# Cached keys fetched page by page and scored with full-height products in a hybrid decoder step

## The chip, the cores and the metric

The kernel runs on one core of a Trainium2 chip. The time is device microseconds (us) from the start of the program to its end, for one execution, with one launch. The core has five engines that run side by side, each through its own instruction queue in order: PE (TensorE, matmuls; PEld is its weight load), DVE (VectorE), ACT (ScalarE), POOL (GpSimd) and SP (SyncE). SP, ACT and POOL also issue DMAs; a queue that issues is written SPq, ACTq or POOLq. An indirect DMA (a gather, one row of memory per partition by a list of indices) is issued by POOL in this kernel.

## The reference

One inference step of a one-layer decoder, with a prompt group (512 tokens) and a sample group (8 sequences of 4 new tokens with 2,048 cached positions each, in 16 pages of 128). The part that the change touches is the sparse attention of the sample group:

```python
ki_past = cki[page_table].reshape(DB, PAST_LEN, IDX_DIM)          # indexer keys, 16 pages a sequence
sc = index_scores(qi, wi, concat([ki_past, ki_new]))               # sum over 8 heads of relu(qi . ki) * wi
_, idx = lax.top_k(sc, 256)                                        # 256 positions of 2,052
k_sel, v_sel = gather(ck, cv by page_table and idx)                # cached keys and values, 2 heads of 64
o = softmax(q . k_sel / 8) @ v_sel                                 # 8 query heads, 4 for each key head
```

Around it stand a gated MLP, the same attention for the prompt, an attention over 256 memory rows, and an expert layer with 16,384 experts (the last two thirds of the time). Everything is in float32; the large projections are three products of halves in a rounded format (fp32r), which are written `mm3`.

## The kernel before, in words

**Phase A** (the first 400 us of the trace) makes the projections, the prompt's attention and the sample group's attention. The projections are the main line: 19 weight tiles of 512 KB (`wA`), each loaded by SP (L232), cut by ACT (L220) and DVE (L224) into a high and a low half, and multiplied on PE (L256 to L258). Two raw tiles and two pairs of halves are held. The other work of phase A runs as *sides*: generators that the main line steps by a declared time, which gives the order in which the program is written. The order on each queue is then drawn by a planner of the tile framework, which plays the program through on a timeline: at every moment a free engine takes the earliest-written instruction that is ready. A buffer of a ring is given out by the planner at the moment its first writer is placed. Once drawn, the order of each queue is fixed, and a queue waits in order.

**Index pages.** The indexer keys of a sequence are 16 pages. `index_rows` (L1317 to L1327) issues four pairs of pages behind each weight tile on SP: a register load (L1324) and a DMA of 32 KB (L1326) for each page, 128 of them in 16 weight tiles. The pages of sequences 4 and 5 and of 6 and 7 lie in two slots of the ring `kv` of three slots; the rest in another ring.

**Index scores.** `sample_scores` multiplies the pages (L1366), and after the sequences 5 and 7 it calls `fetch_kv`, which takes the slot that has come free. Behind that follow the scores of the new positions (L1374 to L1379) and two masks on POOL (L1381, L1382). `sample_select` (L1388) then finds the 256th largest score by 32 rounds of counting on DVE (L1419 to L1431, the count itself is L1420).

**Cached keys and values.** `fetch_kv` fills a slot of the ring `kv` (128 x 2,048, three slots) with the keys of one sequence (the first eight calls) or the values (the last eight), by four gathers of 128 rows of 2 KB (L1283). A row of `cK` is one (head, quarter of 16) of a page: four chunks `e` of the head dimension with 128 positions each. One gather brings four pages, 32 partitions each.

**Scores.** `sample_keys` (L1464 to L1510) runs over the eight sequences: DVE builds the queries spread over four chunks (L1495), PE makes sixteen products on 64 x 64 quarters of the array (L1502), with two PSUM banks, and ACT copies the two banks out (L1506). Behind each sequence stands the next `fetch_kv`. `sample_attend` (L1514) adds the mask of the selected positions (L1541 to L1543), takes the softmax, and multiplies with the values (L1559). Its end closes the memory of the sample group, in which the second half of the prompt's stream is then laid out; so it is a join.

Of the kernel before, what the change touches and what calls it, by code (L numbers as in the profile page):

```python
# [18 lines left out]
P = 128  # L19
NP = 512  # L20
NS = 32
# [30 lines left out]
class Kernel:  # L52
# [173 lines left out]
    def wtile(self, pool, src, kt=KT, n=P):  # L226

        more = pool is self.pw and self.gp is not None and self.RX
        if more:
            self.raws = (self.raws + 1) % (2 + self.RX)  # L230
        raw = self.t(self.gp, [P, kt, n], tag="wraw", bufs=self.RX) if more and self.raws > 1 else self.t(pool, [P, kt, n], tag="wraw", bufs=2)
        load = self.nc.sync.dma_start(raw, src)  # L232
        self.loads += 1
        if self.todo and self.loads > 2:
            self.index_rows(load)
        hi = self.t(pool, [P, kt, n], F32R, tag="whi", bufs=2)
        lo = self.t(pool, [P, kt, n], F32R, tag="wlo", bufs=2)
        self.split(hi, lo, raw)
        return hi, lo


# [1026 lines left out]
    def fetch_kv(self, s2):  # L1268
        n = len(self.kv)
        if n < 16:  # L1270
            kv = self.t(s2, [P, 2048], tag="kv", bufs=self.RING)
            kv = kv.rearrange("p (m x) -> p m x", m=4)
            for m in range(4):
                self.gather(kv[:, m, :], self.I["cV" if n >= 8 else "cK"], self.s_ix[:, n * 4 + m : n * 4 + m + 1])
            self.kv.append(kv)

    RING = 3
# [8 lines left out]
    def pages(self, s1, s2):  # L1286
        nc, I = self.nc, self.I

        pid = self.t(s1, [P, 1])
        for r in range(0, P, 32):  # L1290
            nc.gpsimd.iota(pid[r : r + 32], [[0, 1]], base=0, channel_multiplier=1, allow_small_or_imprecise_dtypes=True)
        pt_i = self.t(s1, [P, P], I32)
        nc.gpsimd.dma_start(pt_i, I["page_table"].rearrange("b n -> (b n)").partition_broadcast(P))
        pf = self.t(s1, [P, P])
        nc.vector.tensor_copy(pf, pt_i)
        self.s_ix = self.t(s1, [P, 64], I32)
        tmp = self.t(s1, [P, 64])
        for u in range(4):
            r = slice(u * 32, u * 32 + 32)

            nc.vector.tensor_scalar(tmp[r, :32].rearrange("p (b c f) -> p b c f", c=2, f=2),
                                    pf[r].rearrange("p (b c v r f) -> p v r b c f", c=2, v=2, r=2, f=2)[:, u % 2, u // 2],
                                    32.0, pid[r], ALU.mult, ALU.add)
            nc.vector.tensor_scalar(tmp[r, 32:], pf[r].rearrange("p (n u) -> p u n", u=4)[:, u], 32.0, pid[r], ALU.mult, ALU.add)
# [12 lines left out]
    def index_rows(self, behind):  # L1317
        nc = self.nc
        src = self.I["cI"].rearrange("(n d) x -> n d x", d=64)
        with self.tc.issue_after(getattr(behind, "ins", behind)):  # L1320
            for pt_i, b, m in self.todo[: self.PAGES]:
                for c in range(2):
                    n = b * 16 + 2 * m + c
                    page = nc.values_load(pt_i[:1, n : n + 1], engines=[mybir.EngineType.SP], min_val=0, max_val=src.shape[0] - 1,  # L1324
                                          skip_runtime_bounds_check_because="a page table holds pages of the pool")
                    nc.sync.dma_start(self.rows[b][c * 64 : c * 64 + 64, m, :], src[bass.ds(page, 1)].rearrange("n d x -> (n d) x"))  # L1326
        self.todo = self.todo[self.PAGES :]  # L1327

    PAGES = 4


    def sample_scores(self, s1, s2):
# [131 lines left out]
    def sample_keys(self, s1, s2):  # L1464
        nc = self.nc

        qb = self.s_qb = self.t(s2, [P, 8, 2, 4, 4])
        nc.vector.memset(qb, 0.0)
        for g in range(2):
            r = slice(g * 64, g * 64 + 64)  # L1470
            for q in range(4):
                nc.vector.tensor_scalar(qb[r, :, g, q], self.s_q[r, q].rearrange("p (b t) -> p b t", t=4), 0.125, None, ALU.mult)

        qs = self.t(s2, [P, 4, 8, 16])
        self.s_room = Room(qs.rearrange("p e b q -> p (e b q)"))
        ps = self.pst("pb")
        for e in range(4):
            perm = self.t(s1, [P, P], tag="qst", bufs=2)
            nc.vector.tensor_copy(perm.rearrange("p (u g d) -> p u g d", u=4, g=2),
                                  self.ident.rearrange("p (g e d) -> p e g d", g=2, e=4)[:, e].unsqueeze(1).to_broadcast([P, 4, 2, 16]))  # L1480
            nc.tensor.matmul(ps[:, e * P : e * P + P], perm, self.s_q.rearrange("p r t -> p (r t)"), start=True, stop=True)
        for e in range(4):
            nc.scalar.activation(qs[:, e].rearrange("p b (r t) -> p r b t", r=4), ps[:, e * P : e * P + P].rearrange("p (r b t) -> p r b t", r=4, b=8),
                                 AF.Copy, scale=0.125)

        own = self.t(s2, [P, 4])
        nc.vector.tensor_reduce(own, self.ident.rearrange("p (r c d) -> p c r d", r=2, d=16), AX.XY, ALU.add)
        yield 1.0
        while not self.indexed:
            yield 1.0  # L1490
        S = [self.t(s1, [P, 4, 512], tag="S8", bufs=2) for _ in range(2)]
        self.s_S = [S[b // 4][:, b % 4, :] for b in range(8)]
        for b in range(8):
            q4 = self.t(s2, [P, 4, 64], tag="q4", bufs=2)
            nc.vector.tensor_tensor(q4.rearrange("p e (c q) -> p e c q", c=4), qs[:, :, b].unsqueeze(2).to_broadcast([P, 4, 4, 16]),  # L1495
                                    own.unsqueeze(1).unsqueeze(3).to_broadcast([P, 4, 4, 16]), ALU.mult)

            pair = [self.pst("pb") for _ in range(2)]
            for e in range(4):
                for o, ps in zip((0, 64), pair):  # L1500
                    for c in range(2):
                        nc.tensor.matmul(ps[c * 64 : c * 64 + 64, : 2 * P].rearrange("p (f x) -> p f x", f=2), q4[o : o + 64, e],  # L1502
                                         self.kv[b][o : o + 64, 2 * c : 2 * c + 2, e * P : e * P + P], start=e == 0, stop=e == 3,
                                         skip_group_check=True, tile_position=(o, c * 64))
            for r, ps in enumerate(pair):
                nc.scalar.copy(self.s_S[b].rearrange("p (m r f x) -> p r f m x", m=4, r=2, f=2)[:, r],  # L1506
                               ps[:, : 2 * P].rearrange("p (f m x) -> p f m x", f=2, m=4))
            self.fetch_kv(s2)
            yield 4.0 * self.SK
        self.keyed = True  # L1510
# [3 lines left out]
    def sample_attend(self, s2, s1):  # L1514
        nc, I = self.nc, self.I
        sel, qb = self.s_sel, self.s_qb
# [38 lines left out]
        def values(b, A):  # L1555
            po = self.pst("pb")
            for m in range(4):
                for c in range(4):
                    nc.tensor.matmul(po[c * NS : c * NS + NS, :P], A[:, m, c, :], self.kv[8 + b][:, c, m * P : m * P + P],  # L1559
                                     start=m == 0, stop=m == 3)  # L1560
# [16 lines left out]
        ps = self.pst("pb")  # L1577
# [4 lines left out]
        A = turn(nxt)  # L1582
        partn = self.t(s1, [P, 2, P], tag="qst", bufs=2)
        for b in range(8):
# [4 lines left out]
            if b == 0:  # L1589
                ps = self.pst("pb")  # L1590
# [3 lines left out]
            if b < 7:  # L1594
                A = turn(nxt)
# [281 lines left out]
```

## Time and profile before

| | |
|---|---|
| median of 3 runs | 1784.9 us (1784.82 to 1789.05) |
| the profiled execution: its own time | 1789.2 us |
| its span in the trace | 1787.5 us |
| mean granted clock of TensorE | 0.959 |
| PE busy | 1661.1 us, 93% |
| DVE busy | 1481.7 us, 83% |
| ACT busy | 864.8 us, 48% |
| POOL busy | 490.4 us, 27% |
| DMA | 460.33 MB, mean 258 GB/s |

The profile is of one execution. Busy time of an engine leaves out the instructions that issue DMAs from SP and ACT, register loads and waits. Matmuls overlap, so a busy PE isn't a PE at its peak. The granted clock is the share of 2.4 GHz that the chip gave PE: 1.0 is 2.4 GHz and 0.5 is 1.2 GHz. A bracket such as `[13.80 <-PE t L1502]` in a timeline says how long the engine had been idle before the instruction and what ended the idle time.

### The profile page before, as it was taken

The numbers are of one execution on the slowest core, as the hardware profiler recorded it, in microseconds if no ns is written. First come the engines' busy times: TensorE is split into PE (matmuls) and PEld (weight loads), VectorE is DVE, ScalarE is ACT, GpSimd is POOL, SyncE is SP. The second block draws the span as 40 slices with busy tenths as digits, with TensorE's granted clock in tenths as the row PEclk, the third lists the DMA queues.
The fourth block names the chain that finished last, engine by engine and source line by source line (L and its number), as shares of the span: only waits on it lengthen the run. The fifth ranks groups of instructions, "written<-read, shape, count | busy, mean of one in ns | idle before, by whom it ended". The sixth has DMA issues, their size and how long they took to land.

```text
span 1787.5 us, 29611 instructions
## 1 busy us (share of the span) xinstructions
PE 1661.1 (93%) x10238; PEld 1465.2 (82%) x10238; DVE 1481.7 (83%) x3654; ACT 864.8 (48%) x1585; POOL 490.4 (27%) x437
## 2 busy tenths in 40 slices
PE   6999989889997998899899998999999999999995
PEld 5879757679886997789889988788788888888884
DVE  4486889755759999999999885799898988878887
ACT  4345776655553335664775674333343333333333
POOL 2100133130000053323223222244333534335343
PEclk8999779889998999899999999999999999999998
DMA  5423436346854597989689789799998999999986
GB/s 178 133 64 111 127 97 200 108 149 212 254 178 122 158 340 267 344 313 344 231 285 312 250 298 299 258 358 331 362 353 302 373 357 325 355 330 323 362 301 234
DMA packets 195205, 460.33 MB, mean 258 GB/s; under 512 B 17976, under 2 KB 98616, under 8 KB 193648
## 3 DMA queue, kind: packets, MB, share of 16 engines
q1 hardware_dynamic: 132928, 241.63, 40.5%
q0 software_dynamic: 53072, 207.71, 32.8%
q10 hardware_dynamic: 9056, 9.11, 1.6%
q8 instruction: 80, 1.31, 0.3%
q14 instruction: 69, 0.57, 0.1%
HBM read 416.11 MB, written 42.05 MB: 256 GB/s over the span
## 4 chain that ended last, share of the span: by engine, by line
PE 66%; DVE 16%; issue 6%; ACT 4%; DMA 4%; SPq 1%; POOL 1%; POOLq 0%; DVEq 0%; ACTq 0%
PE t L256 20%; PE t L258 19%; PE t L257 19%; DVE t L224 3%; DVE t L1742 2%; DMA t<-in_uT 1%; ACT t L220 1%; POOL t L1283 1%; PE t L652 1%; DMA wd<-t 1%; DVE t L940 1%; SPq L1326 1%; DVE t L935 1%; DVE t L931 1%; DVE t L943 1%
## 5 line engine op out<-in xcount | busy, mean ns | idle before, releaser
L258 PE MATMUL t<-t,t 128*128 128x384 f32 (+3 forms) x2544 | 868.8, 345 | 22.9 <-DVE t L224 22.6
L257 PE MATMUL t<-t,t 128*128 128x384 f32 (+3 forms) x2544 | 867.5, 343 | 0.0
L256 PE MATMUL t<-t,t 128*128 128x384 f32 (+3 forms) x2544 | 780.7, 346 | 18.9 <-ACT t L220 15.7
L220 ACT CAST t<-t 128x1024 fp32r<-128x1024 f32 (+4 forms) x512 | 418.1, 841 | 705.6 <-PE t L257 512.8
L224 DVE TENSOR_TENSOR t<-t,t 128x1024 fp32r<-128x1024 f32 (+4 forms) x512 | 487.7, 963 | 146.0 <-ACT t L220 139.5
L258 PEld LDWEIGHTS t<-t,t 128*128 128x128 f32 x2544 | 486.3, 191 | 68.7 <-DVE t L224 28.7
L256 PEld LDWEIGHTS t<-t,t 128*128 128x128 f32 x2544 | 486.0, 192 | 66.1 <-ACT t L220 24.5
L257 PEld LDWEIGHTS t<-t,t 128*128 128x128 f32 x2544 | 486.7, 191 | 37.6 <-issue 5.2
L1283 POOL DMA_INDIRECT t<-in_u,t x160 | 194.3, 1215 | 506.3 <-DVE t L1742 261.3
L1283 POOL DMA_INDIRECT t<-in_v,t x160 | 208.9, 1306 | 305.7 <-DVE t L1747 237.8
L1747 DVE SCALAR_TENSOR_TENSOR t<-t,t,t 128x1024 f32<-128x1024 f32 x160 | 204.6, 1279 | 5.1 <-DMA t<-in_v,t 4.3
L1742 DVE SCALAR_TENSOR_TENSOR t<-t,t 128x1024 f32<-128x1024 f32 x160 | 193.6, 1216 | 9.6 <-DMA t<-in_u,t 9.6
L1088 ACT ACTIVATE t<-t 128x512 f32<-128x512 f32 x96 | 97.5, 1145 | 28.4 <-DMA wd<-t 22.1
L1283 POOL DMA_INDIRECT t<-in_cK,t x32 | 34.0, 1063 | 206.8 <-PE t L1366 146.6
L1224 DVE TENSOR_TENSOR t<-t,t 128x352 f32<-128x352 f32 x128 | 66.4, 519 | 6.0 <-DMA t<-gd 2.5
L1104 ACT ACTIVATE t<-t 128x384 f32<-128x384 f32 x128 | 62.2, 486 | 11.3 <-PE t L258 9.2
L1078 ACT ACTIVATE t<-t,t 128x128 f16<-128x128 f16 x192 | 58.4, 390 | 4.1 <-DVE t L1074 4.1
L1085 PE MATMUL t<-t,t 128*128 128x128 f16 x384 | 51.7, 222 | 6.7 <-DVE t L1075 3.5
L702 ACT ACTIVATE t<-t,t 128x384 f32<-128x384 f32 x64 | 42.7, 667 | 24.8 <-DVE t L699 21.4
L1283 POOL DMA_INDIRECT t<-in_cV,t x32 | 33.1, 1036 | 74.9 <-PE t L1559 51.0
L1086 PE MATMUL t<-t,t 128*128 128x128 f16 x384 | 49.8, 221 | 2.4 <-DVE t L1080 1.8
L1085 PEld LDWEIGHTS <-t 128*128 128x128 f16 x384 | 35.7, 98 | 13.8 <-issue 6.1
(400 smaller groups left out, 1430.3 us busy)
## 6 DMA issues: line engine op xcount, KB each, us to landing
t<-in_uT SPq DMA_DIRECT2D x128, 512.0 KB, 5.6
t<-in_v SPq DMA_DIRECT2D x128, 512.0 KB, 6.1
wd<-t POOLq DMA_DIRECT2D x11, 2048.0 KB, 8.9
t<-wd SPq DMA_DIRECT2D x32, 704.0 KB, 8.4
gd<-t SPq DMA_DIRECT2D x56, 192.0 KB, 4.6
t<-gd SPq DMA_DIRECT2D x56, 192.0 KB, 7.9
t<-in_wA SPq DMA_DIRECT2D x19, 512.0 KB, 4.0
t<-in_wO SPq DMA_DIRECT2D x16, 512.0 KB, 4.0
```

What stands on the lines that cost most here:

```text
L220: self.nc.scalar.copy(hi, x)
L224: self.pin_v = self.nc.vector.tensor_tensor(lo, x, hi, ALU.subtract)
L256: mm(out, ah, bh, start=first, stop=False)
L257: mm(out, ah, bl, start=False, stop=False)
L258: self.pin = mm(out, al, bh, start=False, stop=last)
L1085: nc.tensor.matmul(o, oj[:, x, :], oh[:, x, :], start=True, stop=False)
L1088: nc.scalar.activation(wb[:, :, t : t + 4].rearrange("p i t -> p t i"), ps.rearrange("p (t i) -> p t i", t=4), AF.Copy, scale=1.0 / 2048.0)
L1104: nc.scalar.activation(G, ps, AF.Gelu_apprx_tanh)
L1224: nc.vector.tensor_tensor(q(w)[:, : 4 * NB - 1], self.wp[:, :, i % 4, :], q(G)[:, : 4 * NB - 1], ALU.mult)
L1283: self.nc.gpsimd.indirect_dma_start(out=out, out_offset=None, in_=src, in_offset=bass.IndirectOffsetOnAxis(ap=ix, axis=0))
L1742: nc.vector.scalar_tensor_tensor(r, r, 1.0, hf, ALU.mult, ALU.mult, accum_out=a[:, k : k + 1])
L1747: nc.vector.scalar_tensor_tensor(acc, r, a[:, k : k + 1], acc, ALU.mult, ALU.add)
```

## The change

The keys of a sequence come by sixteen gathers, one for each page, of 128 rows of 512 B: the row of partition (e, head, d) is chunk `e` of row (head, d) of that page, so the 128 partitions hold the 128 numbers of a position and the free axis the 2,048 positions. The index list grows from 64 to 160 columns, made by one DVE instruction for the keys and four for the values. The queries are put into that order by one product with a permutation (before: four), and each sequence takes four products with all 128 rows of the array, 32 columns and 512 positions each, into one PSUM bank, and one copy by ACT. The spread queries per sequence (L1495) and their mask are gone. The values come as before.

Of the four pairs of index pages behind a weight tile, three stay on SP and one is issued from ScalarE's queue, written behind the tile's split.

```diff
@@ wtile
-            self.index_rows(load)
+            self.index_rows(load, self.nc.sync, mybir.EngineType.SP, self.PAGES)
         hi = self.t(pool, [P, kt, n], F32R, tag="whi", bufs=2)
         lo = self.t(pool, [P, kt, n], F32R, tag="wlo", bufs=2)
         self.split(hi, lo, raw)
+        if self.todo and self.loads > 2:
+            self.index_rows(self.pin_v, self.nc.scalar, mybir.EngineType.Activation, 1)
         return hi, lo
@@ fetch_kv
-            kv = kv.rearrange("p (m x) -> p m x", m=4)
-            for m in range(4):
-                self.gather(kv[:, m, :], self.I["cV" if n >= 8 else "cK"], self.s_ix[:, n * 4 + m : n * 4 + m + 1])
+            if n < 8:
+                for m in range(16):
+                    self.gather(kv[:, m * P : m * P + P], self.I["cK"].rearrange("n (e x) -> (n e) x", e=4), self.s_ix[:, n * 16 + m : n * 16 + m + 1])
+            else:
+                for m in range(4):
+                    i = P + (n - 8) * 4 + m
+                    self.gather(kv[:, m * 512 : m * 512 + 512], self.I["cV"], self.s_ix[:, i : i + 1])
@@ pages
+            nc.gpsimd.iota(pid4[r : r + 32], [[0, 1]], base=r // 32, channel_multiplier=4, allow_small_or_imprecise_dtypes=True)
...
+        nc.vector.tensor_scalar(tmp[:, :P], pf, float(P), pid4, ALU.mult, ALU.add)
...
@@ index_rows
-    PAGES = 4
+    PAGES = 3
@@ sample_keys
-        qs = self.t(s2, [P, 4, 8, 16])
...
-        for e in range(4):
-            perm = self.t(s1, [P, P], tag="qst", bufs=2)
...
-            nc.tensor.matmul(ps[:, e * P : e * P + P], perm, self.s_q.rearrange("p r t -> p (r t)"), start=True, stop=True)
...
-        nc.vector.tensor_reduce(own, self.ident.rearrange("p (r c d) -> p c r d", r=2, d=16), AX.XY, ALU.add)
+        nc.tensor.matmul(ps[:, :256], perm, qb.rearrange("p b g r t -> p (b g r t)"), start=True, stop=True)
+        room = self.t(s2, [P, 512])
+        q3 = room[:, :256].rearrange("p (b q) -> p b q", b=8)
+        nc.scalar.copy(room[:, :256], ps[:, :256])
...
-            q4 = self.t(s2, [P, 4, 64], tag="q4", bufs=2)
...
-            pair = [self.pst("pb") for _ in range(2)]
-            for e in range(4):
-                for o, ps in zip((0, 64), pair):
-                    for c in range(2):
-                        nc.tensor.matmul(ps[c * 64 : c * 64 + 64, : 2 * P].rearrange("p (f x) -> p f x", f=2), q4[o : o + 64, e],
-                                         self.kv[b][o : o + 64, 2 * c : 2 * c + 2, e * P : e * P + P], start=e == 0, stop=e == 3,
-                                         skip_group_check=True, tile_position=(o, c * 64))
-            for r, ps in enumerate(pair):
-                nc.scalar.copy(self.s_S[b].rearrange("p (m r f x) -> p r f m x", m=4, r=2, f=2)[:, r],
-                               ps[:, : 2 * P].rearrange("p (f m x) -> p f m x", f=2, m=4))
+            ps = self.pst("pb")
+            for c in range(4):
+                nc.tensor.matmul(ps[c * NS : c * NS + NS, :], q3[:, b], self.kv[b][:, c * 512 : c * 512 + 512],
+                                 start=True, stop=True)
+            nc.scalar.copy(self.s_S[b].rearrange("p (m u x) -> p u m x", m=4, u=4), ps.rearrange("p (u m x) -> p u m x", u=4, m=4))
             self.fetch_kv(s2)
```

## Rows read from the trace of the kernel before

**Rows 1.** The page, busy time of PE: us, share of the span, instructions.

```profile
PE 1661.1 (93%) x10238; PEld 1465.2 (82%) x10238; DVE 1481.7 (83%) x3654; ACT 864.8 (48%) x1585; POOL 490.4 (27%) x437
```

**Rows 2.** Windows: busy us (instructions) PE, PEld, DVE, ACT, POOL; PEclk, DMA share, GB/s.

```profile
200.00:250.00 50.00, 38.65 (x186) 24.16 (x185) 42.56 (x239) 42.70 (x129) 14.30 (x16) 0.56 0.32 93
250.00:300.00 50.00, 49.74 (x424) 36.80 (x423) 46.56 (x189) 29.64 (x71) 20.00 (x18) 1.00 0.54 165
300.00:350.00 50.00, 44.38 (x300) 35.35 (x300) 41.76 (x148) 31.79 (x66) 2.29 (x2) 0.90 0.43 132
```

**Rows 3.** Chain that ended last, 148 to 198 us: start, us, what.

```profile
148.48 0.27 SPq L1324
148.94 0.47 SPq L1326
...
179.39 2.64 DMA t<-in_cI
...
182.15 15.00 issue
...
197.38 0.94 POOL t L1283
```

**Rows 4.** Timelines of SP, ACT and PE, 147 to 177 us: start, us, engine, line.

```profile
147.93 23.25 SPq L1326 DMA_DIRECT2D t<-in_cI  x24
171.28 0.53 SPq L232 DMA_DIRECT2D t<-in_wA  x1
...
175.22 1.04 ACT L220 CAST t<-t 128x1024 fp32r<-128x1024 f32 x1 [5.81 <-DMA t<-in_wA]
...
176.31 0.39 PE L256 MATMUL t<-t,t 128*128 128x256 f32 x1 [2.13 <-ACT t L220]
```

**Rows 5.** Chain that ended last, shares by line, 200 to 260 and 260 to 300.

```profile
by line: ACT t L702 19.5%; issue 8.6%; PE t L1502 6.2%; DVE t L1420 6.0%; PE t L256 4.8%; ACT t L871 4.6%; ACT L871 4.3%; PE t L257 3.4%; PE t L258 3.2%; PE t L861 3.1%; ACT t L874 2.9%; PE t L887 2.8%; DVE t L705 2.0%; DVE t L867 1.7%; POO
by line: DVE t L224 17.3%; DVE t L1420 14.0%; PE t L1502 9.4%; issue 6.4%; DVE t L867 5.5%; PE t L861 3.8%; ACT t L871 3.3%; DVE t L1421 3.1%; DVE t L1431 3.0%; PE t L256 3.0%; PE t L257 3.0%; PE t L258 3.0%; DVE t L1419 2.9%; DVE t L1422 2
```

**Rows 6.** Timeline of PE, products of keys (L1502) and of values (L1559).

```profile
253.19 1.94 PE L1502 MATMUL t<-t,t 64*64 64x256 f32 x16
...
283.25 1.96 PE L1502 MATMUL t<-t,t 64*64 64x256 f32 x32
...
354.20 1.08 PE L1559 MATMUL t<-t,t 128*32 128x128 f32 x32
```

**Rows 7.** Instructions by line: duration ns min/median/max, first and last start; gathers' busy us, mean.

```profile
L1495 DVE TENSOR_TENSOR t<-t,t x8: 414/417/418, 210.4 to 286.0; 128x256 f32<-128x256 f32 x8
L1479 DVE COPY t<-t x4: 150/209/222, 187.7 to 206.5; 128x128 f32<-128x128 f32 x4
L1506 ACT COPY t<-t x16: 349/372/379, 220.1 to 297.4; 128x256 f32<-128x256 f32 x16
L1283 POOL DMA_INDIRECT t<-in_cK,t x32 | 34.0, 1063 | 206.8 <-PE t L1366 146.6
```

**Rows 8.** Timeline of POOL, 45 to 271 us.

```profile
48.92 1.85 POOL L1283 DMA_INDIRECT t<-in_cK,t  x1 [0.30 <-issue]
197.38 0.94 POOL L1283 DMA_INDIRECT t<-in_cK,t  x1 [146.60 <-PE t L1366]
...
202.33 0.46 POOL L1381 TENSOR_SCALAR_AFFINE_SELECT t<-t 32x32 f32<-32x32 f32 x1
...
270.10 0.94 POOL L1283 DMA_INDIRECT t<-in_cK,t  x1 [0.30 <-issue]
```

**Rows 9.** Counting rounds on DVE (by line), and the end of the selection (chain).

```profile
L1420 DVE SCALAR_TENSOR_TENSOR t<-t,t,t x32: 769/784/787, 208.0 to 322.2; 128x544 f32<-128x544 f32 x32
...
338.45 0.65 DVE t L1456
...
340.84 0.43 PE t L1541
```

**Rows 10.** Timeline of ACT: casts of weight tiles with the idle time before them, a DMA issue.

```profile
53.72 1.05 ACT L220 CAST t<-t 128x1024 fp32r<-128x1024 f32 x1 [5.02 <-PE t L257]
...
143.20 1.05 ACT L220 CAST t<-t 128x1024 fp32r<-128x1024 f32 x1 [0.74 <-PE t L257]
...
159.02 0.39 ACTq L442 DMA_DIRECT2D out_vT<-t  x1
```

More of the change, by code (lines that the diff above doesn't have):

```diff
@@ L1287, in pages @@
         nc, I = self.nc, self.I
-        pid = self.t(s1, [P, 1])
+        pid, pid4 = self.t(s1, [P, 1]), self.t(s1, [P, 1])
         for r in range(0, P, 32):
             nc.gpsimd.iota(pid[r : r + 32], [[0, 1]], base=0, channel_multiplier=1, allow_small_or_imprecise_dtypes=True)
+            nc.gpsimd.iota(pid4[r : r + 32], [[0, 1]], base=r // 32, channel_multiplier=4, allow_small_or_imprecise_dtypes=True)
         pt_i = self.t(s1, [P, P], I32)
@@ L1295, in pages @@
         nc.vector.tensor_copy(pf, pt_i)
-        self.s_ix = self.t(s1, [P, 64], I32)
-        tmp = self.t(s1, [P, 64])
+        self.s_ix = self.t(s1, [P, P + 32], I32)
+        tmp = self.t(s1, [P, P + 32])
+        nc.vector.tensor_scalar(tmp[:, :P], pf, float(P), pid4, ALU.mult, ALU.add)
         for u in range(4):
             r = slice(u * 32, u * 32 + 32)
[L1301 to L1304, printed above, removed]
+            nc.vector.tensor_scalar(tmp[r, P:], pf[r].rearrange("p (n u) -> p u n", u=4)[:, u], 32.0, pid[r], ALU.mult, ALU.add)
         nc.vector.tensor_copy(self.s_ix, tmp)
@@ L1314, in pages, with index_rows @@
             self.fetch_kv(s2)
-    def index_rows(self, behind):
+    def index_rows(self, behind, queue, engine, n):
         nc = self.nc
@@ L1320, in index_rows @@
         with self.tc.issue_after(getattr(behind, "ins", behind)):
-            for pt_i, b, m in self.todo[: self.PAGES]:
+            for pt_i, b, m in self.todo[:n]:
                 for c in range(2):
-                    n = b * 16 + 2 * m + c
-                    page = nc.values_load(pt_i[:1, n : n + 1], engines=[mybir.EngineType.SP], min_val=0, max_val=src.shape[0] - 1,
+                    i = b * 16 + 2 * m + c
+                    page = nc.values_load(pt_i[:1, i : i + 1], engines=[engine], min_val=0, max_val=src.shape[0] - 1,
                                           skip_runtime_bounds_check_because="a page table holds pages of the pool")
-                    nc.sync.dma_start(self.rows[b][c * 64 : c * 64 + 64, m, :], src[bass.ds(page, 1)].rearrange("n d x -> (n d) x"))
-        self.todo = self.todo[self.PAGES :]
-    PAGES = 4
+                    queue.dma_start(self.rows[b][c * 64 : c * 64 + 64, m, :], src[bass.ds(page, 1)].rearrange("n d x -> (n d) x"))
+        self.todo = self.todo[n:]
+    PAGES = 3
     def sample_scores(self, s1, s2):
@@ L1472, in sample_keys @@
                 nc.vector.tensor_scalar(qb[r, :, g, q], self.s_q[r, q].rearrange("p (b t) -> p b t", t=4), 0.125, None, ALU.mult)
-        qs = self.t(s2, [P, 4, 8, 16])
-        self.s_room = Room(qs.rearrange("p e b q -> p (e b q)"))
+        perm = self.t(s1, [P, P], tag="qst", bufs=2)
+        nc.vector.tensor_copy(perm.rearrange("p (e g d) -> p e g d", e=4, g=2), self.ident.rearrange("p (g e d) -> p e g d", g=2, e=4))
         ps = self.pst("pb")
-        for e in range(4):
-            perm = self.t(s1, [P, P], tag="qst", bufs=2)
-            nc.vector.tensor_copy(perm.rearrange("p (u g d) -> p u g d", u=4, g=2),
-                                  self.ident.rearrange("p (g e d) -> p e g d", g=2, e=4)[:, e].unsqueeze(1).to_broadcast([P, 4, 2, 16]))
-            nc.tensor.matmul(ps[:, e * P : e * P + P], perm, self.s_q.rearrange("p r t -> p (r t)"), start=True, stop=True)
-        for e in range(4):
-            nc.scalar.activation(qs[:, e].rearrange("p b (r t) -> p r b t", r=4), ps[:, e * P : e * P + P].rearrange("p (r b t) -> p r b t", r=4, b=8),
-                                 AF.Copy, scale=0.125)
-        own = self.t(s2, [P, 4])
-        nc.vector.tensor_reduce(own, self.ident.rearrange("p (r c d) -> p c r d", r=2, d=16), AX.XY, ALU.add)
+        nc.tensor.matmul(ps[:, :256], perm, qb.rearrange("p b g r t -> p (b g r t)"), start=True, stop=True)
+        room = self.t(s2, [P, 512])
+        q3 = room[:, :256].rearrange("p (b q) -> p b q", b=8)
+        nc.scalar.copy(room[:, :256], ps[:, :256])
+        self.s_room = Room(room)
         yield 1.0
@@ L1493, in sample_keys @@
         for b in range(8):
-            q4 = self.t(s2, [P, 4, 64], tag="q4", bufs=2)
-            nc.vector.tensor_tensor(q4.rearrange("p e (c q) -> p e c q", c=4), qs[:, :, b].unsqueeze(2).to_broadcast([P, 4, 4, 16]),
-                                    own.unsqueeze(1).unsqueeze(3).to_broadcast([P, 4, 4, 16]), ALU.mult)
-            pair = [self.pst("pb") for _ in range(2)]
-            for e in range(4):
-                for o, ps in zip((0, 64), pair):
-                    for c in range(2):
-                        nc.tensor.matmul(ps[c * 64 : c * 64 + 64, : 2 * P].rearrange("p (f x) -> p f x", f=2), q4[o : o + 64, e],
-                                         self.kv[b][o : o + 64, 2 * c : 2 * c + 2, e * P : e * P + P], start=e == 0, stop=e == 3,
-                                         skip_group_check=True, tile_position=(o, c * 64))
-            for r, ps in enumerate(pair):
-                nc.scalar.copy(self.s_S[b].rearrange("p (m r f x) -> p r f m x", m=4, r=2, f=2)[:, r],
-                               ps[:, : 2 * P].rearrange("p (f m x) -> p f m x", f=2, m=4))
+            ps = self.pst("pb")
[3 more added lines that the diff above has]
+            nc.scalar.copy(self.s_S[b].rearrange("p (m u x) -> p u m x", m=4, u=4), ps.rearrange("p (u m x) -> p u m x", u=4, m=4))
             self.fetch_kv(s2)
@@ L1558, in values @@
                 for c in range(4):
-                    nc.tensor.matmul(po[c * NS : c * NS + NS, :P], A[:, m, c, :], self.kv[8 + b][:, c, m * P : m * P + P],
+                    nc.tensor.matmul(po[c * NS : c * NS + NS, :P], A[:, m, c, :], self.kv[8 + b][:, c * 512 + m * P : c * 512 + m * P + P],
                                      start=m == 0, stop=m == 3)
```

## The prediction

> **What bounds the kernel now.** I read the page first: PE is busy for 93% of the span [rows 1], so what shifts the end of phase A shifts the end of the kernel, and nothing behind the join at its end hides it. The change lies in phase A, so I then read it in windows. From 200 to 250 us PE is busy 38.65 of 50 us at a granted clock of 0.56 while DVE and ACT are busy over 42; from 250 to 300 PE and DVE are both nearly full [rows 2]. The chain that ended last says which of them is late where. Before 198 it runs for some 30 us along SP's index pages, then from the last page to a gather on POOL [rows 3]. From 200 to 260 it is ACT and DVE with 6.2% of the key products, from 260 to 300 mostly DVE with 9.4% of them [rows 5]. The reader is to see that the path of the sample group (index pages, index scores, two masks on POOL, 32 counting rounds on DVE, then the attention) sets the end of phase A, with DVE the engine that has the least room, and that PE's products are only a part of it. Last I read the timelines of the queues that the change loads: POOL idle for 146.60 us before 197.38 [rows 8], ACT with 5.02 us before a cast early and 0.74 us later [rows 10].
>
> **The change part by part.**
>
> *Index pages off SP.* A page on SP costs a register load of 0.27 and a DMA issue of 0.47 us [rows 3]; 24 of them took 23.25 us, so 0.97 each with the gaps [rows 4]. 32 of 128 pages leave SP: 31 us of its queue. That matters once. The pages of sequences 6 and 7 wait for a slot and then go out in one run of 24, and the weight tile behind it is issued only at 171.28; ACT has by then waited 5.81 us for it and PE 2.13 [rows 4]. With one in four gone the run is at most 18 pages, 5.8 us shorter, which covers ACT's wait. PE gains 2.1 at least where it waited; at most the chain moves by 5.8; nothing, if the order around it shifts. I take -2, the row of PE's own wait.
>
> *The same pages on ACT.* 32 issues at 0.39 (an issue of ACT's own [rows 10]) plus the load of 0.27, up to SP's 0.97: 21 to 31 us, or 1.3 to 1.9 per weight tile. Behind them queue the casts of the tiles, for which PE waits. Early on 5.02 us of idle time in front of a cast covers this; where only 0.74 is left it doesn't, and some 1.2 us is exposed. The pages have to be written behind the split but don't depend on it, so the planner can place them in ACT's idle time. Bounds 0 and +5 (four late tiles of 1.2); I take +1.
>
> *Products on PE.* A sequence's products take 1.96 us where all four quarters of the array run together, and 1.94 for each half where they don't [rows 6]. The new ones go through 32 columns of the array like the value products, with the same 512 columns in each of the four groups, and those take 1.08 [rows 6]. On the chain stand 6.2% of 60 and 9.4% of 40 us [rows 5], 7.5 us; 1.08 for 1.96 saves 45% of it: -3.4. Bounds 0 (PE isn't late there) and -7.5.
>
> *DVE.* Eight query instructions of 0.417 go and three permutation copies of about 0.2 [rows 7]: 3.9 us on an engine that is busy 89 of 100 us [rows 2]. I take -3; bounds 0 and -3.9. The index list at the start has fewer DVE instructions too, and lies in front of everything: nothing.
>
> *ACT's copies.* Sixteen copies of 0.372 become eight of twice the length [rows 7]. Between no gain (twice the time each) and -3.0 (the same time each) I take 0, since their place on the chain is counted with the products.
>
> *The gathers.* Four gathers occupy POOL from 197.38 to 202.33, 4.95 us, 1.24 each [rows 8]; the mean of all 32 is 1.063 plus 0.30 between them [rows 7, 8], 1.36. Sixteen take 20 to 22 us. The first two sequences' lie before 197 (before, the second ended at about 50), and 40 to 44 us fit into POOL's 146.60 us of idle time: nothing. The other six start when the slot of the index pages comes free, at 197.38, and their 96 gathers take 119 to 131 us: to 317 or 329, and a landing of about 2.64 (that of a page, the nearest row [rows 3]) behind it. Before, the last started at 270.10 [rows 8]. The attention begins at 340.84, when the selection has ended [rows 9]. So 9 to 21 us of cover remain and the gathers cost nothing by themselves, if the products that wait for them stand late enough in PE's queue. With the cover gone each further 0.1 us per gather costs 9.6 us.
>
> *What queues behind them.* The two masks on POOL that end the index scores stood behind the third sequence's four gathers, at 202.33 [rows 8]. They are written behind `fetch_kv` and are ready later than the slot, so they will now stand behind sixteen: 12 gathers more, 14.9 us. The first count waits for them. The 32 rounds start from 208.0 to 322.2, one in 3.68 us [rows 9], so four rounds are lost at the front. DVE has idle time to catch up, 7.4, 3.4 and 8.2 us in the three windows [rows 2], and other work to pull forward meanwhile. Bounds 0 (caught up, or index scores that end earlier because SP is less loaded) and +15 (all carried). I take half, +7.5.
>
> Here a rule speaks against the change. The gathers' rows show 1.063 us on average and 1.85 at the longest of those shown, while DVE is nearly full [rows 7, 8]. The Trainium skill (SBUF — State Buffer, section "SBUF: two separate sides") says that a DVE instruction in a two-port mode locks GpSimd out of the port through which it writes the descriptors of its DMAs. By the mean row the sum stays as above; if the rule took hold so that each gather cost the longest row, it would be the third rival below.
>
> The sum: -2 + 1 - 3.4 - 3 + 0 + 7.5 = +0.1. The profiled execution took 1789.2 (span 1787.5), 4.3 above the median of 1784.9; made on its own time the sum gives 1789.3, and carried to the median 1785.
>
> **The rivals.**
>
> *Faster: the masks don't move.* If the index pages arrive earlier and the planner places sequence 7's index products some 8 to 10 us sooner, or DVE catches up fully, the +7.5 falls to about 0 and the rest stands: -2 + 1 - 3.4 - 3.9 - 1 (some of ACT's copies) = -9, 1776. For it speaks the run of 24 pages on the chain; against it that sequence 7's pages had landed at 182.15 and POOL was still released only at 197.38 [rows 3], so the pages weren't the last thing there.
>
> *Slower: the whole delay is carried.* DVE has 3.4 us free of 50 between 250 and 300, so four rounds that weren't made before can't be made there. Then the selection ends 15 us later: -2 + 1 - 3.4 - 3 + 15 = +8, 1793. It decides from the point where DVE's work in front of the first count runs out.
>
> *Slower: the gathers end last.* At 1.46 us per gather, (340.84 - 197.38 - 2.64 - 0.8) / 96, the keys come when the selection ends; above it POOL sets the attention. At the longest row, 1.85 + 0.30, 96 gathers take 206 us, the keys come at 407 and the kernel would take about 66 - 8 = 58 more, 1843; at 1.6 it would be some 13 - 8 + 7.5, 1797. A milder form: the products stand too early in PE's queue and hold up the projections behind them. Against it: the mean of 1.36.
>
> **How the numbers follow.** No change that can be told, 0.38: the likeliest, 1785, with its own range of 1780 to 1790. Faster 0.30 (1776), the whole delay 0.20 (1793), the gathers last 0.12 (1797 to 1843). Within 0.3% of 1784.9 (5.4 us, about what three runs can tell from no change) is "same". So faster 0.30, same 0.38, slower 0.32. The range for 8 in 10 takes the middle of both outer cases with their bounds: down to 1771 (the three gains nearer their bounds, the masks unmoved), up to 1799; what it leaves out is the stronger form of the last rival and the luckiest of the first.
>
> **What would show it.** Sixteen gathers in a row on POOL from near 197 and the first mask only behind them, near 217; the first count near 222 where it was at 208.0, and the last round's distance from 322.2 telling how much was caught up. No weight tile that waits for SP's pages near 171. Key products of about 1.1 us, the last after 317. No cast on ACT that is late by a page's issue. The prediction would be wrong if the first count didn't move, if the last one moved by the full 15, if PE waited for a gather, or if a shift came from behind phase A, where nothing is changed and only the planner's order could differ.

## The result and the profile after

The changed kernel takes 1903.98 us (median of 4 runs, 1900.41 to 1908.14), the kernel before beside it 1785.33 (1784.82 to 1789.05): a ratio of 1.0659, 95% interval 1.0626 to 1.0692. The forecast was 1785, with a range of 1771 to 1799; the kernel is 119 us slower.

The page's busy times of the changed kernel answer to [rows 1]. PE, DVE and ACT do the same work as before to within a microsecond; POOL has 100 instructions and 102 us more.

```profile
PE 1660.2 (87%) x10040; PEld 1454.5 (76%) x10040; DVE 1480.9 (78%) x3639; ACT 864.6 (45%) x1574; POOL 592.8 (31%) x537
```

So the work of PE, DVE and ACT did not grow; these engines stand more. Two views say where. The first is a line that both kernels have, the attention over the memory rows behind the join at the end of the sample group (L565 before, L567 after), by line (shortest, median and longest in ns, then the first and the last start):

```profile
L565 PE MATMUL t<-t,t x32: 379/379/774, 399.3 to 506.3; 128*128 128x256 f32 x32
```

```profile
L567 PE MATMUL t<-t,t x32: 379/379/774, 520.5 to 627.7; 128*128 128x256 f32 x32
```

It starts 121.2 us later; the spans differ by 1905.1 - 1787.5 = 117.6. All of the loss lies in phase A. The second view is the windows, first two of the kernel before, then those of the changed kernel (columns as in [rows 2], which hold the others of before):

```profile
0.00:50.00 50.00, 32.54 (x217) 29.68 (x218) 21.97 (x66) 19.89 (x35) 16.45 (x31) 0.90 0.58 185
50.00:100.00 50.00, 50.00 (x310) 40.25 (x308) 28.33 (x73) 16.79 (x30) 0.77 (x1) 1.00 0.38 112
```

```profile
0.00:50.00 50.00, 19.55 (x120) 16.15 (x120) 15.93 (x52) 17.52 (x32) 18.88 (x33) 0.84 0.53 159
50.00:100.00 50.00, 37.89 (x230) 35.86 (x229) 14.27 (x33) 7.00 (x8) 21.64 (x26) 0.75 0.35 98
...
250.00:300.00 50.00, 17.68 (x81) 10.47 (x81) 13.59 (x86) 16.77 (x56) 33.67 (x35) 0.64 0.17 44
300.00:350.00 50.00, 23.19 (x122) 14.62 (x122) 17.89 (x80) 16.85 (x42) 23.21 (x24) 0.70 0.22 63
276.70:321.40 44.70, 0.00 (x0) 0.00 (x0) 0.07 (x1) 0.00 (x0) 30.29 (x33) 0.50 0.18 48
```

Where POOL is busy with gathers, PE, DVE and ACT are all emptier than before, and for 44.70 us nothing but POOL works; the clock falls to 0.50 there, the 1.2 GHz level. POOL's timeline in the changed kernel answers to [rows 8]:

```profile
225.81 1.28 POOL L1289 DMA_INDIRECT t<-in_cK,t  x1 [142.39 <-PE t L1370]
...
246.25 0.94 POOL L1289 DMA_INDIRECT t<-in_cK,t  x1 [0.30 <-issue]
247.20 0.28 POOL L1385 TENSOR_SCALAR_AFFINE_SELECT t<-t 32x32 f32<-32x32 f32 x1
...
255.96 0.95 POOL L1289 DMA_INDIRECT t<-in_cK,t  x1 [8.14 <-PE t L1494]
...
315.80 0.94 POOL L1289 DMA_INDIRECT t<-in_cK,t  x1 [0.31 <-issue]
```

The third sequence's gathers start 28.43 us later than in [rows 8], sixteen of them stand before the mask, and from 255.96 to 316.7 there are 48 in a row, most of them 1.25 us apart. The counting rounds and the first product of the attention answer to [rows 9], by line and in PE's timeline:

```profile
L1424 DVE SCALAR_TENSOR_TENSOR t<-t,t,t x32: 776/785/805, 253.3 to 450.6; 128x544 f32<-128x544 f32 x32
```

```profile
460.59 0.61 PE L1530 MATMUL t<-t,t 128*128 128x512 bf16 x1
```

A count takes as long as before (785 ns), but the 31 intervals take 197.3 us, not 114.2: 6.36 each instead of 3.68. The 119.8 us by which the attention starts later are thus 28.4 (before the third sequence), 16.4 more for the mask, 0.5 to the first count, 83.1 in the rounds, less 8.7 behind the last.

What a stall looks like is seen at 274 us, in the timeline of all engines of the changed kernel:

```profile
273.85 0.44 PE L889 MATMUL t<-t,t 128*128 128x128 f32 x2
...
314.55 0.95 POOL L1289 DMA_INDIRECT t<-in_cK,t  x1 [0.30 <-issue]
315.80 0.94 POOL L1289 DMA_INDIRECT t<-in_cK,t  x1 [0.31 <-issue]
321.47 0.27 ACT L890 COPY t<-t 128x128 f32<-128x128 f32 x1 [46.46 <-remote]
321.47 0.42 DVE L869 CUSTOM_DVE_ANT_0 t<-t,t 128x256 f32<-128x256 f32 x1 [44.70 <-remote]
...
321.96 1.22 PE L863 MATMUL t<-t,t 64*128 64x256 f32 x2 [47.67 <-DVE t L869]
```

ACT's copy (L890) takes what PE's transposes (L889) have written. They ended by 274.3; the copy starts at 321.47, together with DVE's instruction that waits for another product of PE, and only some 5 us after the last gather of the row. The profile calls the releaser "remote", since no instruction ends there; no other core runs. Nothing that these instructions need was being computed in the 44.70 us, and by the DMA view of the stretch from 276.8 to 323 only the gathers' own queue moved data, so no late transfer was holding them either.

### The profile page after: what moved, and what is told of

The parts are those of the page before. It is cut to its first block, busy times and chain, and to the rows that moved or that the text cites. A ratio compares the mean times of both kernels' runs of the same rounds, so it can differ in the third digit from the quotient of the medians.

```text
span 1905.1 us, 29313 instructions
## 1 busy us (share of the span) xinstructions
PE 1660.2 (87%) x10040; PEld 1454.5 (76%) x10040; DVE 1480.9 (78%) x3639; ACT 864.6 (45%) x1574; POOL 592.8 (31%) x537
## 4 chain that ended last, share of the span: by engine, by line
PE 61%; DVE 18%; issue 7%; DMA 5%; ACT 4%; another core or an unknown queue 4%; POOL 1%; ACTq 0%; SPq 0%; DVEq 0%; POOLq 0%
PE t L260 18%; PE t L258 18%; PE t L259 17%; DVE t L224 4%; DVE t L1731 2%; DMA t<-in_u,t 1%; DMA t<-in_uT 1%; PE t L654 1%; DVE t L942 1%; ACT t L220 1%; DVE t L937 1%; DMA wd<-t 1%; POOL t L1289 1%; DVE t L1736 1%
## 5 line engine op out<-in xcount | busy, mean ns | idle before, releaser
L260 PEld LDWEIGHTS t<-t,t 128*128 128x128 f32 x2544 | 488.3, 192 | 86.7 <-DVE t L224 32.6
L259 PEld LDWEIGHTS t<-t,t 128*128 128x128 f32 x2544 | 488.9, 192 | 44.6 <-issue 12.1
L1289 POOL DMA_INDIRECT t<-in_v,t x160 | 214.1, 1338 | 301.9 <-DVE t L1736 237.4
L1289 POOL DMA_INDIRECT t<-in_cK,t x128 | 128.4, 1003 | 219.8 <-PE t L1370 142.4
L863 PE MATMUL t<-t,t 64*128 64x128 f32 (+3 forms) x64 | 21.9, 536 | 78.3 <-DVE t L869 67.9
L863 PEld LDWEIGHTS t<-t,t 64*128 64x128 f32 x64 | 8.7, 216 | 85.6 <-DVE t L869 70.0
L869 DVE CUSTOM_DVE_ANT_0 t<-t,t 128x128 f32<-128x128 f32 (+3 forms) x32 | 15.2, 488 | 54.4 <-remote 51.0
L1087 PE MATMUL t<-t,t 128*128 128x128 f16 x384 | 51.7, 222 | 5.3 <-DVE t L1077 2.6
```

What stands on the lines that cost most here:

```text
L259: mm(out, ah, bl, start=False, stop=False)
L260: self.pin = mm(out, al, bh, start=False, stop=last)
L1289: self.nc.gpsimd.indirect_dma_start(out=out, out_offset=None, in_=src, in_offset=bass.IndirectOffsetOnAxis(ap=ix, axis=0))
```

## The experiments

Where a run below has no ratio, it is one execution. The kernel before itself took from 1777.69 to 1793.72 us beside these runs, so differences of less than some 15 us between such runs are not read. The runs e3 to e6, e8 and e15 fetch other pages or keys than the reference needs, as their expectations say; they are made for the time alone.

**Which half of the change.** Two theories. A: the index pages on ScalarE's queue, with its register loads, are what delays the engines. B: the sixteen gathers of a sequence are.

```diff
 # e1: the change, all pages on SP
-        if self.todo and self.loads > 2:
-            self.index_rows(self.pin_v, self.nc.scalar, mybir.EngineType.Activation, 1)
...
-    PAGES = 3
+    PAGES = 4
 # e2: the kernel before, with the two lines that e1 takes out and PAGES = 3
 # e3: the change, ScalarE's pages without a register load
+                    if queue is nc.scalar:
+                        queue.dma_start(rows, src[i : i + 1].rearrange("n d x -> (n d) x"))
+                        continue
 # e4: the change, four gathers of 2 KB rows for the keys
-                for m in range(16):
-                    self.gather(kv[:, m * P : m * P + P], ...)
+                for m in range(4):
+                    self.gather(kv[:, m * 512 : m * 512 + 512], self.I["cK"], ...)
```

> The changed kernel with all four pairs of index pages behind a weight tile back on SP; gathers and products as changed. Theory A (the pages that ScalarE's queue issues, with a register load of their own on that engine, are what delays the semaphores of every engine): the stall of 44.70 us from 276.70 goes, PE's idle share from 250 to 350 comes back to that of the kernel before, and the time is 1780 to 1800 us. Theory B (the sixteen gathers of 512 B for each sequence, 128 in place of 32, hold up all engines while POOL issues them): the stall stays and the time stays within 10 us of 1904.

Measured: 1903.52 us, ratio 1.0651 (1.0609 to 1.0694). The stall stays too: PE, DVE and ACT stand from 280.04 to 325.37.

> The kernel before with one of four pairs of index pages moved to ScalarE's queue and nothing else; four gathers of 2 KB a sequence. Theory A: slower by several per cent, 1840 to 1905 us, with stretches in which all engines stand while POOL gathers. Theory B: 1780 to 1795 us, as the index pages were priced in the prediction (-2 + 1).

Measured: 1776.85 us, ratio 0.994 (0.9919 to 0.996): some 3 us below the range of theory B, far from that of A.

> The changed kernel, but ScalarE's queue loads pages at fixed addresses (those of the table's positions, not the table's pages), so that ScalarE makes no register load and its page DMAs are ordinary ones. Theory A in the form that the register load or the address from a register is the cause: 1780 to 1800 us. Theory A in the form that any DMA of ScalarE's queue in this place is the cause, or theory B: 1895 to 1910 us.

Measured: 1899.1 us. The register loads on ScalarE are not the cause; whether other DMAs on its queue are, this run can't tell from theory B.

> The changed kernel, with the keys fetched by four gathers of 2 KB rows (rows of the values' index list, so the scores are not those of the reference's keys); products and index pages on ScalarE as changed. Theory A: 1860 to 1905 us, the engines still stand while POOL gathers. Theory B: 1780 to 1795 us, and the stretch from 250 to 350 us is full again.

Measured: 1792.89 us, beside 1790.37 for the kernel before on that chip. So theory A has fallen: without ScalarE's pages the loss stays, with them alone there is a gain, and four gathers in place of sixteen take 111 us off. Per gather that is left out this is 111.1 / 96 = 1.16 us, nearly the whole 1.25 us for which POOL issues it. The size does not hang on the one execution of e4: the same pair with all pages on SP, e1 against e15 (below), differs by 1903.52 - 1788.08 = 115.4 us, over 4 and 8 runs on one chip.

**Which property of the gathers.** Their number, their rows of 512 B, or the number of rows.

```diff
 # e5: sixteen of 32 rows x 2 KB
-                for m in range(16):
...
+                for m in range(4):
+                    for u in range(0, P, 32):
+                        self.gather(kv[u : u + 32, m * 512 : m * 512 + 512], self.I["cK"], self.s_ix[:32, ...])
 # e6: four of 128 rows x 512 B, all products read that quarter
-                for m in range(16):
+                for m in range(4):
 # e7: three fills behind every fourth gather
+                    if m % 4 == 3:
+                        for _ in range(3):
+                            nc.gpsimd.memset(idle, 0.0)
 # e8: eight of 128 rows x 1 KB
+                for m in range(8):
+                    self.gather(kv[:, m * 256 : m * 256 + 256], ...)
```

> The changed kernel with sixteen gathers a sequence of 32 rows of 2 KB each in place of 128 rows of 512 B: as many instructions, as many bytes, a quarter of the rows (the rows are not the right ones, so the scores are not the reference's). Theory B1 (the number of gathers issued in a row on POOL is what holds up the other engines' semaphores): the stretch from 250 to 350 stays empty, 1880 to 1905 us, less if one gather of 32 rows is shorter. Theory B2 (rows of 512 B are): 1775 to 1795 us. Theory B3 (the rows that POOL has to write out one after another, 2,048 a sequence in place of 512): 1775 to 1795 us.

Measured: 1920.79 us, 16 above the range of theory B1. The rows are a quarter and of 2 KB, the bytes those of the kernel before, and the loss is all there: it goes with the number of instructions. In the timeline, PE, DVE and ACT stand from 280.21 to 305.72 beside a row of gathers that are even shorter (0.86 us).

> The changed kernel with only four of the sixteen gathers of a sequence, 128 rows of 512 B each, and all four products read that quarter (three quarters of the keys are left out). Theory B1 and B3: 1770 to 1790 us, no stretch in which all engines stand. Theory B2: stalls as long as the gathers last, a quarter of the loss or more, 1800 to 1815 us.

Measured: 1796.21 us, between the two ranges, and beside 1780.95 for one execution of the kernel before on that chip. Four gathers of 2 KB took 1792.89, on another chip. In its trace PE, DVE and ACT nowhere stand together for more than 2 us between 10 and 430 us. So rows of 512 B alone don't make the stalls; by that execution beside it they can cost some 15 us at most.

> The changed kernel with eight gathers a sequence, 128 rows of 1 KB each (the same bytes, half the gathers and rows of the change, twice those of the kernel before; the keys are in the wrong order). A dose between four (1792.9) and sixteen (1904.0): if the loss grows with the number of gathers, 1810 to 1840 us; if it begins only when a row of gathers is longer than some length that lies between the 20 in a row of the kernel before and the 48 of the change, 1780 to 1800 us (24 in a row here).

Measured: 1823.2 us, 30.3 above four gathers, or 0.95 us for each of the 32 more: inside the range for a loss that grows with the number. The one longer stall begins in the row of 24 gathers (218.0 to 248.7) and ends 3.5 us behind it; its window in this run:

```profile
243.10:252.20 9.10, 0.00 (x0) 0.00 (x0) 0.00 (x0) 0.00 (x0) 4.42 (x5) 0.50 0.29 86
```

> The changed kernel with three fills of a spare tile by POOL (about 0.5 to 0.7 us each) behind every fourth gather of the keys, so that no more than four gathers stand in a row; all keys are fetched. If an uninterrupted row of gathers is what starves the semaphores (B1 in that form), the semaphores get through in the pauses, the stall of 44.70 us breaks up into pieces of some 5 us, and much of the loss goes: 1800 to 1850 us. If each gather costs the others a fixed time, or the rows do (B2, B3), the loss stays: 1890 to 1930 us.

Measured: 1923.04 us. This tested nothing: in the timeline all 96 fills stand before 123 us, where the planner found POOL idle, and the row from 269.7 to 329.9 still has 48 gathers without a gap.

**Whether it is the row or each gather.** The pauses again, now tied in place: the gathers behind a pause are held behind it in POOL's order.

```diff
 # e10: a copy that waits for the landing behind every fourth (e9: every eighth, m % 8 == 7)
+                    with ExitStack() as st:
+                        if self.pause is not None:
+                            st.enter_context(self.tc.issue_after(self.pause.ins))
                         self.gather(kv[:, m * P : m * P + P], ...)
+                    if m % 4 == 3:
+                        self.pause = nc.gpsimd.tensor_copy(seen[:, :1], kv[:, m * P : m * P + 1])
 # e14: six fills behind every fourth, held in place, no wait for a landing
+                        self.pause = self.gather(kv[:, m * P : m * P + P], ...)
+                    if m % 4 == 3:
+                        for _ in range(6):
+                            with self.tc.issue_after(self.pause.ins):
+                                self.pause = nc.gpsimd.memset(seen, 0.0)
```

> The changed kernel with all its 128 gathers of the keys, but behind every eighth POOL copies one column of what has just been gathered and the next gathers stand behind that copy, so that POOL waits for the landing (some 2.6 us) and no more than eight gathers stand in a row. The 96 late gathers then last from about 225 to 380 instead of 357. If it is the length of an uninterrupted row that holds up the other engines (eight and twelve in a row cost nothing in the kernel before, sixteen do): no stretch longer than 3 us in which PE, ACT and DVE all stand, the keys come some 40 us behind the end of the selection, 1810 to 1840 us. If every gather above those of the kernel before costs about its own 1.2 us wherever it stands: 1895 to 1935 us.

Measured: 1860.72 us, 43 less than the change, and in neither range: above what the row's length alone should give (1810 to 1840) and below a fixed cost for each gather (1895 to 1935).

> The same with a pause behind every fourth gather: 24 pauses among the 96 late gathers, keys until about 410. Length of a row as the cause: engines as busy as in the kernel before until the selection has ended, then a wait for the keys of some 70 us, 1835 to 1865 us. A fixed cost per gather: 1900 to 1940 us, with stalls as in the change.

Measured: 1845.41 us, as forecast for the length of a row: the kernel that takes longer over its gathers is 59 us faster. Its waits (us in total, times, longest) name what is left, the keys that come late:

```profile
PE t L1500 <- DMA t<-in_cK,t: 50.5, 12, 7.0
```

> As the run with a pause behind every fourth gather (1845.41 us), but the pause is six fills of a spare tile by POOL, held in their place, some 3.2 us, and POOL waits for no landing. If it is enough that the engines get a gap between rows of gathers: within 15 us of 1845, no stretch of more than 6 us in which PE, ACT and DVE stand. If it matters that the gathers in flight have landed before the next ones go out: stalls as in the change, 1885 to 1925 us.

Measured: 1854.92 us, inside the 15 us that were set around e10, and no stretch in which PE, DVE and ACT all stand is longer than 5.94 us: the gap itself is enough, the landing needn't be waited for. POOL's timeline shows the pause, and the counts by line show what it does:

```profile
200.49 2.26 POOL L1284 MEMSET t<- 128x512 f32 x4
202.91 1.03 POOL L1297 DMA_INDIRECT t<-in_cK,t  x1 [0.16 <-issue]
```

```profile
L1432 DVE SCALAR_TENSOR_TENSOR t<-t,t,t x32: 767/784/787, 204.3 to 322.3; 128x544 f32<-128x544 f32 x32
```

The selection starts 3.7 us earlier than in the kernel before and ends where it did [rows 9], with the gathers of the change beside it. What this run loses is again the wait for the keys, 70.2 us in all (its waits):

```profile
PE t L1502 <- DMA t<-in_cK,t: 70.2, 14, 7.9
```

One round of counting puts the runs in order. Each interval is (last start - first start) / 31 from the counts' row of that run; the gaps are from POOL's timeline.

| run | gathers in a row while counting | one round, us |
|---|---|---|
| before [rows 9] | 4, 4, 4 with gaps of 2.9 and 1.3 us; 24 us later 8 | 3.68 |
| e14 | 4, gaps of 3.7 us | 3.81 |
| e15 (below) | 12, then 4 to 8 | 3.90 |
| e4 | 12, then 4 | 4.14 |
| e10 | 4, gaps of some 2.4 us | 4.49 |
| e8 | 24 and 16 | 5.00 |
| e9 | 8, gaps of some 2.5 us, 24 at the end | 5.19 |
| the change | 48, then 16 twice | 6.36 |

It isn't a sharp length, and it isn't the share of the time either: by POOL's timelines gathers fill 60% of the counting in e14 and 33% in e4, yet e4, with its row of twelve, has the longer round. Long rows and short gaps go with slow rounds. That e10, with the same rows of four as e14, is slower by its shorter gaps fits this; no run changes the gap alone.

**The other terms, and a faster version.** The index pages alone were the fastest run so far, so a second pair was moved; and the products were tried alone, with all pages on SP and four gathers for the keys.

```diff
 # e13: e2 with two pairs on ScalarE
-            self.index_rows(self.pin_v, self.nc.scalar, mybir.EngineType.Activation, 1)
+            self.index_rows(self.pin_v, self.nc.scalar, mybir.EngineType.Activation, 2)
-    PAGES = 3
+    PAGES = 2
 # e15: e4 with all pages on SP
```

> The kernel before with two of four pairs of index pages on ScalarE's queue (one: 1776.85 us). If what helped there is that SP's run of 24 pages in front of a weight tile gets shorter, another few us come off: 1768 to 1776 us. If ScalarE's casts become the next bound, it goes back to 1777 to 1787 us.

Measured: 1781.0 us, ratio 0.9977 (0.9959 to 0.9996), beside 0.994 for one pair, with intervals that touch: the second pair brings no further gain. It isn't lost in phase A: in the trace of e13, its fastest execution, the line behind the join (L567) starts at 391.8, 7.5 us earlier than in the kernel before. So ScalarE's casts did not become the bound there; what takes the rest stays open.

> The kernel before with the new products, queries and copies alone: four gathers of 2 KB a sequence (rows of the values' list, so other keys than the reference's) and all index pages on SP. The prediction's terms for products, DVE and copies, -3.4 - 3 + 0: 1776 to 1784 us against 1785.3. If the path that these lie on isn't where they were costed, or the rows of gathers that the planner now puts together (twelve in a row in the run with four gathers, 1792.9) take back what they give: 1785 to 1797 us.

Measured: 1788.08 us beside 1782.23, ratio 1.0034 (1.0018 to 1.0049): no gain, a small loss.

## Why the prediction was wrong

**The gathers: this step failed.** The prediction took 1.24 to 1.36 us for a gather, found room for 96 of them until the attention, and wrote down nothing. The price of one was right (mean below, and 0.30 between two), and the gathers did not end last: the last key gather of the changed kernel ended near 381, the selection's last count began at 450.6. What was wrong is the premise that a gather costs only its own engine. By lines, the gathers of the changed kernel:

```profile
L1289 POOL DMA_INDIRECT t<-in_cK,t x128 | 128.4, 1003 | 219.8 <-PE t L1370 142.4 <-issue 37.2 <-PE t L1494 27.9
```

In place of 0 the term measured 111 us (the change against e4; 115.4 by e1 against e15). The same error hides the first two sequences: "40 to 44 us fit into POOL's idle time" is true of POOL, but PE's timeline of the changed kernel, beside their gathers from 13.3 to 34.0, reads

```profile
22.90 0.29 PE L259 MATMUL t<-t,t 128*128 128x288 f32 x1
24.44 0.29 PE L260 MATMUL t<-t,t 128*128 128x288 f32 x1 [1.25 <-issue]
26.54 0.29 PE L258 MATMUL t<-t,t 128*128 128x288 f32 x1 [1.81 <-issue]
28.70 0.37 PE L259 MATMUL t<-t,t 128*128 128x256 f32 x1 [1.88 <-issue]
30.79 0.37 PE L260 MATMUL t<-t,t 128*128 128x256 f32 x1 [1.72 <-issue]
```

One matmul in 2.1 us, where the lines in front of them come each 0.1 to 0.3 us. In the first two windows above PE is busy 13.0 and 12.1 us less. That the 28.43 us by which the third sequence started late come from these rows is shown by e14: with the same 32 early gathers, but gaps behind every fourth, the third sequence starts 4 us earlier than in the kernel before. POOL's timeline of e14:

```profile
193.30 1.28 POOL L1297 DMA_INDIRECT t<-in_cK,t  x1 [105.80 <-PE t L1378]
```

**What queues behind them: right in kind.** The mask fell behind sixteen gathers; from the first gather to the mask it took 21.39 us instead of 4.95, 16.4 more where 14.9 was worked out. But half of it was to be caught up by DVE, and nothing was: the rounds themselves became slower.

**The rivals.** "The gathers end last" was on the right side and wrong in mechanism: POOL's gathers were not slow and PE's wait for keys does not show in the change; its 1843 was also 61 us short. The waits for the keys that it spoke of appear only in e9, e10 and e14, where pauses make the gathers later. In "the whole delay is carried" the delay was right and the 83 us in the rounds missing.

**The rule of the Trainium skill** (SBUF — State Buffer, section "SBUF: two separate sides") that DVE in a two-port mode locks GpSimd out of its descriptor writes would have made gathers longer. They were not: 1.003 us on average in the changed kernel, against 1.063 before. They took 0.94 to 0.95 in the stall, where DVE stood, and up to 1.62 beside working engines between 225 and 381 us; that would fit the rule, but no run here shows that DVE's mode is the reason. Here POOL slowed the others, not they POOL; and a lock between POOL and DVE alone would not explain the stall, since ACT's copy (L890) reads only what PE had written. The same section of the Trainium skill says that transfers and compute cannot slow each other through memory; the runs agree as far as bytes go, since e4, e5 and the change move as many bytes of keys and only the number of gathers tells.

**Index pages.** The two terms, -2 and +1, by e2: SP's run in front of the weight tile has 17 pages, and the tile goes out at 166.79 instead of 171.28 [rows 4]; no wait of PE between 140 and 180 is left. SP's timeline of e2:

```profile
150.08 16.61 SPq L1328 DMA_DIRECT2D t<-in_cI  x17
166.79 0.53 SPq L232 DMA_DIRECT2D t<-in_wA  x1
```

Its join stands at 396.4, 2.9 us earlier, for -1 predicted. The two profiled executions differ by 12.5 us, so most of that lies behind the join. There PE's granted clock differs as well as the order: over the whole span it is 0.964 in e2 and 0.959 before, and the same 10238 instructions of PE take 1649.7 and 1661.1 us. How much of the 0.6% is the pages' own stays open.

**Products, DVE, ACT.** The sizes were right where the products run together, their worth was not. In e15 a sequence's products take some 1.07 us. In the changed kernel those of the last sequences stand apart in PE's order, one of the four at a time and as long as all four together, and PE is busy 21.4 us with the key products, against 10.4 in e15 (by lines; 32.6 before). In PE's timelines, e15 first:

```profile
235.14 1.07 PE L1492 MATMUL t<-t,t 128*32 128x512 f32 x8
```

```profile
426.40 1.04 PE L1494 MATMUL t<-t,t 128*32 128x512 f32 x2
```

Eight copies of ACT take 0.579 each, 4.6 us where sixteen took 6.0; one permutation copy of 0.151 is left. Yet in e15, which has all of it and no more gathers than before, the rounds take 3.90 us each and the time is 0.34% up instead of 6.4 us down. In that run the planner sets twelve gathers in a row (211.0 to 226.5) where the kernel before has three rows of four with gaps. That these take back what the products give fits the table above, but no run separates it.

**The list of signs.** No weight tile waited for SP's pages, the last key products stood behind 317, no cast was late by a page, and PE waited for no gather. A key product took 1.04 us, but for a quarter of a sequence where the four stood apart. The first count came at 253.3 and not 222, and the last moved by 128.4 where 15 was the bound.

## What to carry to other kernels

An engine that is off the critical path is not free: before filling its idle time with instructions that issue DMAs by index, look in the trace at what the other engines do beside a row of them, and price the number of such instructions and the gaps between them, not the bytes. Fewer gathers with longer rows, or gaps between small groups of them, kept the others going here. Here a layout that halves the time of the products was worth nothing, because it quadruples the gathers; the only part of this change that measured as a gain is the index pages on ScalarE (0.994 with one pair).

## What the runs showed of the hardware

Gathers issued without a gap hold up what the other engines tell each other: PE's results of 274.3 us were taken up at 321.47, 5 us after a row of 48, while each gather by itself kept its 0.95 us. The effect goes with the number of gather instructions and not with their rows or bytes (16 of 32 rows cost as much as 16 of 128). It shows plainly where 16 or more stand in a row (one round of counting 5.00 us with rows of 24 and 16, 6.36 with 48) or eight with gaps of some 2.5 us (5.19), and all but vanishes from the selection with gaps of 3.7 us after every four (118.0 us for 31 rounds against 114.2, and 197.3 without gaps). PE also issued only one matmul in 2.1 us beside a row of 16, with no wait that the profile names. By which path the gathers do this, no run shows.
